# A hybrid SSD and gated-linear-attention trunk: the meta tokens' values from one 32-column operand, and more raw buffers with earlier loads in the Strassen part

## The chip, the cores and the metric

The kernel runs on one core of a Trainium2 chip. The metric is the time of one execution in microseconds of the device. Below, PE is TensorE (PEld its weight loads), DVE is VectorE, ACT is ScalarE, POOL is GpSimd, and SP is SyncE, whose queue issues most of the loads. L966 is line 966 of the kernel.

## The reference, cut to what matters

One layer over 2048 tokens of width 1024, with 16 learned meta tokens ahead of them, in float32:

```python
u = rmsnorm(hres, norm_w)
proj = jnp.einsum('bld,dn->bln', u, w_in)
z, xbc, dt_raw, q, k, v, g_gla, a_lr, merge_g = split_cols(proj, IN_WIDTHS)
...   # convolution and SSD branch: y_ssd
o_m, st_m = gla_chunked(q[:, :m], k[:, :m], v[:, :m], log_a[:, :m], N_META, st0)
o_r, _ = gla_chunked(q[:, m:], k[:, m:], v[:, m:], log_a[:, m:], GLA_CHUNK, st_m)
...   # norm and gate: y_gla
branch_proj = jnp.einsum('blnc,ncd->blnd', branches, w_branch)
gates = jax.nn.sigmoid(merge_g.reshape(b, l, N_BRANCH, D_MODEL))
merged = jnp.sum(gates * branch_proj, axis=2)
return hres + jnp.einsum('bld,de->ble', merged, w_out)
```

After the layer comes a final rmsnorm, and the meta tokens are dropped. Of the meta tokens the gated branch needs only what they leave in its state, `st_m`: for each of the four heads the sum over the 16 tokens of the decayed key times the value.

## The kernel before, in words

**Products.** A float32 number is split into a high and a low part (`h`, `lo`), both of type float32r, and a product is three matmuls: high by high, high by low, low by high. The helper `accum` issues them, at L189, L190 and L191, so nearly every matmul of the kernel carries one of these three lines. A tile is named by its tag: `whl` is a weight split in two, `u` the normalised input split in two.

**First part (to about 1500 us).** Four blocks of 512 tokens. In each block four groups of the SSD branch and four heads of the gated branch are projected and scanned, as generators that PE's program order interleaves. In block 0 the 16 meta tokens ride along. For the values of a head, `gla_values` calls `proj_tok`: for each of eight slices of the inner dimension the four chunks of 128 tokens are the stationary operand, and 256 columns of weights are the moving one. In block 0 a fifth chunk, 128 tokens from token 0 on, goes the same way into bank `pv5` (tag `pt`); only its first 16 rows are read, into `vm`. In `gla_scan` the meta tokens' decayed keys (`kd[:, :META]`) are transposed on PE (L771), copied (L773) and multiplied with `vm` (L785), which gives the state `s_gla`.

**Second part (from about 1504 us).** Seven stages, one after the other: gate 0, branch 0 and branch 1 for the first 1024 tokens (56, 28 and 28 products), the same three for the second 1024, and the output stage (56 products). Each stage is a matrix product by Strassen's scheme in Winograd's form: per column pair `n` seven products, in the order `PS = (1, 2, 6, 7, 5, 3, 4)`, two column pairs at a time, so 1, 1, 2, 2, 6, 6, 7, 7, 5, 5, 3, 3, 4, 4. A product is twelve matmuls of 512 columns (`product`, four slices by three passes). The work around it:

- *Right operands.* Each stage needs 28 tiles, four for each of the seven products. `load_b` (L966) loads a raw tile (tag `br`, 5 buffers, SP's queue), `prep_b` splits it: the high part on ACT (L971), the low part on DVE (L972). DVE's instruction frees the raw buffer.
- *Left operands.* `load_a` (L978) loads four raw tiles per column pair (tag `ar`, 8 buffers, SP's queue); POOL forms their sums (L986 to L989), `prep_a` splits each (ACT L995, DVE L996).
- *Snapshots.* Products 1, 6, 5 and 3 add up in one bank (`psa`). After 1, 6 and 5 ACT copies the running sum out (`sn`, L1012), and PE may go on in that bank only then. Between 1 and 6, and between 6 and 5, three other products lie; between 5 and 3 there is one.

PE's and SP's orders are written out: `at(pos, ...)` puts every load and preparation at a position counted in products, and SP issues in that order, each instruction waiting for its own buffer and holding back all behind it. A stage's right operands are prepared from 12 positions ahead of the stage on, 0.8 positions apart, and loaded 3.2 positions ahead of that. The orders on ACT, DVE and POOL are set by a scheduler, at build time. Besides, SBUF holds 16 KB per partition (the default) as scratch for descriptors of DMAs that POOL issues.

Of the kernel before, what the change touches and what calls it, by code (L numbers as in the profile page):

```python
# [19 lines left out]
NCH = BLK // P  # L20
SG = 4
# [7 lines left out]
NC1 = 6  # L29
# [11 lines left out]
def trunk_kernel(ctx: ExitStack, tc: tile.TileContext, xm, xmt, w_feat, w_tok, w_zm, w_br, w_o,  # L41
                 cf32, cmsk, pvec, fnw, hvec, gw2, out):
    nc = tc.nc
# [84 lines left out]
    wk = first.enter_context(tc.tile_pool(name="wk", bufs=2))  # L128
# [58 lines left out]
    def accum(ps, stat, mov, first, last, **kw):  # L187
        (sh, sl), (mh, ml) = stat, mov
        nc.tensor.matmul(ps, sh, mh, start=first, stop=False, **kw)  # L189
        nc.tensor.matmul(ps, sh, ml, start=False, stop=False, **kw)  # L190
        nc.tensor.matmul(ps, sl, mh, start=False, stop=last, **kw)  # L191
# [10 lines left out]
                    accum(ps[:, :n], (h[:, cs], lo[:, cs]), moving(kt, a, n), kt == 0, kt == KT - 1)  # L202
        return pss

    def proj_tok(key, src, u, starts, banks, width=256, per=2, sub=None):

        nq = KT // per
        opened = set()  # L210
        for q0 in range(0, nq, 2):
            if q0 == nq // 2:
                yield
            ws = [load_w(f"{key}_{q}", src[:, q * per * width:(q + 1) * per * width]) for q in (q0, q0 + 1)]
            for i, ((bk, ps), a) in enumerate(zip(banks, starts)):
                c0 = sub if sub is not None and i >= NCH else 0
                for k2 in range(2 * per):
                    kt = q0 * per + k2
                    h, lo = ws[k2 // per]
                    cs = slice(k2 % per * width + c0, (k2 % per + 1) * width)  # L220
                    accum(ps[:, c0:width], tuple(t[:, kt, a:a + P] for t in u),
                          (h[:, cs], lo[:, cs]), bk not in opened, kt == KT - 1, skip_group_check=True)
                    opened.add(bk)
# [149 lines left out]
    def new_block(b, u):  # L373
        o = Block()
        o.b, o.u = b, u
        o.m0 = META if b == 0 else 0
        o.tt = o.m0 + BLK
        o.segs_all = [(0, o.tt // 2), (o.tt // 2, o.tt // 2)] if b == 0 else [(0, BLK)]
        o.segs_real = [(o.m0, BLK)]
        o.starts = [o.m0 + c * P for c in range(NCH)]  # L380
        o.chunks = ([(0, META)] if o.m0 else []) + [(a, P) for a in o.starts]
        o.ci0 = 1 if o.m0 else 0
        o.nck = len(o.chunks)
        for nm in ("tkd", "tkc", "ntc", "wde", "ecu", "dec"):
            setattr(o, nm, mk(bpool, [P, 5, NH], F32, nm, bufs=1))
        o.cumd = mk(dpool, [NH, BLK], F32, "cumd")
        o.g_all = mk(bpool, [P, GH, META + BLK], F32, "g_all")
        o.alr = mk(bpool, [P, 5, 48], F32, "alr")
        o.mov = lambda kt, a, n: tuple(t[:, kt, a:a + n] for t in u)
        return o  # L390
# [256 lines left out]
    def gla_values(o, h):  # L647
        m0 = o.m0
        vh = mk(wk, [P, NCH, 256], F32R, "tok4", bufs=NT4)
        vl = mk(wk, [P, NCH, 256], F32R, "tok4", bufs=NT4)  # L650
        vm = None
        pss, places = halves_of(pj, "pj")
        if m0:
            vm = mk(wk, [P, 256], F32, "c1", bufs=NC1)[:META]
            pv5 = bank(pt, "pt")
            places.append((2, pv5[:, :256]))
        yield from proj_tok(f"v{h}", w_tok[SG + h], o.u, o.starts + [0] * o.ci0, places)
        if m0:
            nc.scalar.activation(vm, pv5[:META, :256], AF.Copy)
        for r, ps in enumerate(pss):  # L660
            split(*[t[:, 2 * r:2 * r + 2].rearrange("p c f -> p (c f)") for t in (vh, vl)], ps)
        return (vh, vl), vm
# [36 lines left out]
    def gla_scan(o, h, qs, kf, got):  # L699
# [68 lines left out]
        yield  # L768
        if m0:
            ps = bank(pt, "pt")  # L770
            nc.tensor.transpose(ps[:META, :P], kd[:, :META], ident)  # L771
            btm = mk(wk, [P, P], F32, "bt")
            nc.scalar.activation(btm[:META], ps[:META, :P], AF.Copy)  # L773
        ps = bank(pt, "pt")
        for c in range(NCH):
            nc.tensor.transpose(ps[:, c * P:(c + 1) * P], kd[:, m0 + c * P:m0 + (c + 1) * P], ident)
# [5 lines left out]
        yield  # L782
        if m0:
            ps = bank(pc, "pc")
            nc.tensor.matmul(ps[:, :256], btm[:META], got["v"][1], start=True, stop=True)  # L785
            nc.vector.tensor_copy(s_gla[:, h], ps[:, :256])
        level_out(32)
        level_in(8)
# [162 lines left out]
    class Stage:  # L951
# [9 lines left out]
        def load_b(self, p, j):  # L961
            src = {1: lambda j: self.braw(j, 0), 2: lambda j: self.braw(4 + j, 0), 3: lambda j: self.braw(4 + j, 1),
                   4: lambda j: self.sums[1][j][:, 1], 5: lambda j: self.sums[0][j][:, 1],
                   6: lambda j: self.sums[1][j][:, 0], 7: lambda j: self.sums[0][j][:, 0]}[p]
            raw = self.braws[p, j] = mk(rpl, [P, BLK], F32, "br", bufs=5)
            nc.sync.dma_start(raw, src(j))  # L966

        def prep_b(self, p, j):
# [5 lines left out]

        def load_a(self, n):
            def raw(i, j):
                t = mk(rpl, [P, 4, P], F32, "ar", bufs=8)
                nc.sync.dma_start(t, self.araw(n, i, j))  # L978
                return t

            if n not in self.a:
                self.a[n] = raw(0, 0), raw(0, 1), raw(1, 0)
                return
            (a11, a12, a21), a22 = self.a[n], raw(1, 1)
            s1, s2, s4 = [mk(rpl, [P, 4, P], F32, "as", bufs=6) for _ in range(3)]
            nc.gpsimd.tensor_tensor(s1, a21, a22, op=ALU.add)  # L986
            nc.gpsimd.tensor_tensor(s2, s1, a11, op=ALU.subtract)
            nc.gpsimd.tensor_tensor(a21, a11, a21, op=ALU.subtract)
            nc.gpsimd.tensor_tensor(s4, a12, s2, op=ALU.subtract)  # L989
            self.a[n] = {1: a11, 2: a12, 3: s4, 4: a22, 5: s1, 6: s2, 7: a21}  # L990
# [71 lines left out]
    def out_stage():  # L1062
        fns, res, ssq, done = [], {}, {}, set()

        def fetch(n, i, t):
            r0 = (2 * n + i) * P
            res[n, i, t] = r = io()
            nc.sync.dma_start(r, xm[META + r0:META + r0 + P, t * BLK:(t + 1) * BLK])

        def use(n, i, t, ps, snap):  # L1070
            r0 = (2 * n + i) * P
            r = res[n, i, t]
            done.add((n, i, t))
            x = total(ps, snap)
            nc.vector.scalar_tensor_tensor(r, x, 0.5, r, op0=ALU.mult, op1=ALU.add)
            if (n, i) not in ssq:
                ssq[n, i] = mk(spl, [P, 2], F32, "ssf")
            jk = mk(spl, [P, BLK], BF16, "junk", bufs=1)
            nc.scalar.activation(jk, r, AF.Square, accum_out=ssq[n, i][:, t:t + 1])
            if (n, i, 1 - t) in done:  # L1080
                while len(fns) < 2:
                    fns.append(mk(rpl, [P, BLK], F32, "br", bufs=5))
# [13 lines left out]

    stages = []
# [24 lines left out]
    for si, st in enumerate(stages):  # L1122
        for q in range(28):
            p, j = PS[q // 4], q % 4
            pos = begins[si] - 12 + 0.8 * q if si else -0.99 + 0.2 * (q // 4) if q < 16 else 2 * (q // 4 - 4)
            at(pos - (3.2 if si else 0.1), lambda st=st, p=p, j=j: st.load_b(p, j))
            at(pos, lambda st=st, p=p, j=j: st.prep_b(p, j))
    for i, (st, n, p) in enumerate(order):
        if p in USES and st.fetch:
# [108 lines left out]
```

## Time and profile before

| | |
|---|---|
| time, median of 3 runs (lowest, highest) | 2315.93 us (2313.01, 2315.98) |
| profiled execution, its own time | 2308.46 us |
| its span, first to last instruction | 2306.7 us |
| PE busy | 2232.1 us, 97% |
| DVE, ACT, POOL busy | 1609.6, 1121.4, 683.6 us |
| moved by DMA | 515.89 MB, 224 GB/s on average |
| mean granted clock of TensorE | 0.990 |

All durations come from the profiled execution. It took 7.47 us less than the median of the runs; a sum made against its time is carried over to the median by that difference. PE is busy nearly always, so what counts is which matmuls there are, and the few places where PE stands still.

### The profile page before, as it was taken

What the parts mean: (1) busy time and instruction counts of PE and PEld (TensorE: products, weight loads), DVE (VectorE), ACT (ScalarE), POOL (GpSimd) and SP (SyncE); (2) the same over time, 40 slices, a digit from 0 to 9 for tenths busy, and PEclk for the clock granted to TensorE, in tenths of its full rate; (3) what the DMA queues carried; (4) which work ended last, traced back from release to release, by engine and by line L of the source; (5) the groups of instructions that cost most, each with busy time, mean ns of one, the idle gap of its engine ahead of it and who ended that gap; (6) DMA issues with size and microseconds to landing.
All of it is one profiled execution on the core that took longest, in us unless ns stands there. A gap on an engine that the chain in (4) does not pass through costs nothing.

```text
span 2306.7 us, 36436 instructions
## 1 busy us (share of the span) xinstructions
PE 2232.1 (97%) x12631; PEld 1949.0 (84%) x12631; DVE 1609.6 (70%) x3136; ACT 1121.4 (49%) x2508; POOL 683.6 (30%) x675
## 2 busy tenths in 40 slices
PE   6899999999999999999999999989999999999998
PEld 6899988888888989888988898778787788787886
DVE  5786766687775677676578656664779855778966
ACT  5565554454444445444455334454644545554443
POOL 3344433122221222222122100145424264423341
PEclk9999999999999999999999999999999999999999
DMA  7766865667786676786667644465767866778653
GB/s 260 234 220 219 289 229 205 203 204 230 257 284 193 204 223 213 253 286 215 205 216 230 215 163 156 151 224 200 252 238 261 280 215 217 255 255 273 226 186 110
DMA packets 300809, 515.89 MB, mean 224 GB/s; under 512 B 27616, under 2 KB 143584, under 8 KB 300624
## 3 DMA queue, kind: packets, MB, share of 16 engines
q1 hardware_dynamic: 221840, 422.15, 56.5%
q10 hardware_dynamic: 78624, 90.89, 11.2%
q8 instruction: 99, 1.62, 0.3%
q14 instruction: 86, 0.70, 0.1%
q0 software_dynamic: 160, 0.52, 0.1%
HBM read 366.26 MB, written 147.19 MB: 223 GB/s over the span
## 4 chain that ended last, share of the span: by engine, by line
PE 64%; DVE 12%; DMA 12%; issue 6%; ACT 4%; POOL 1%; SPq 1%; ACTq 0%; DVEq 0%; POOLq 0%
PE pj L189 11%; PE pj L191 11%; PE pj L190 11%; PE psa L189 4%; PE psa L190 4%; PE psa L191 4%; DMA acc<-in_xmt 2%; PE psb L190 2%; PE psb L189 2%; PE psb L191 2%; DMA br<-br_t 2%; PE pc L594 2%; PE pc L758 1%; DVE b L972 1%; PE psc L190 1%
## 5 line engine op out<-in xcount | busy, mean ns | idle before, releaser
L189 PE MATMUL pj<-u,whl 128*128 128x512 f32 (+1 forms) x1184 | 446.0, 377 | 9.5 <-ACT acc L504 4.5
L191 PE MATMUL pj<-u,whl 128*128 128x512 f32 (+1 forms) x1184 | 430.7, 364 | 0.8 <-POOL whl L177 0.8
L190 PE MATMUL pj<-u,whl 128*128 128x512 f32 (+1 forms) x1184 | 430.1, 363 | 0.0
L189 PE MATMUL pj<-whl,u 128*128 128x256 f32 (+1 forms) x992 | 288.7, 291 | 2.4 <-ACT u L252 2.2
L191 PE MATMUL pj<-whl,u 128*128 128x256 f32 (+1 forms) x992 | 282.2, 285 | 0.2 <-DVE u L257 0.2
L190 PE MATMUL pj<-whl,u 128*128 128x256 f32 (+1 forms) x992 | 282.0, 284 | 0.0
L189 PE MATMUL psa<-b,a 128*128 128x512 f32 x640 | 254.0, 397 | 16.4 <-ACT sn L1012 16.2
L189 PEld LDWEIGHTS pj<-u,whl 128*128 128x128 f32 x1184 | 224.5, 190 | 48.4 <-ACT acc L504 5.4
L190 PE MATMUL psa<-b,a 128*128 128x512 f32 x640 | 253.1, 395 | 2.0 <-DVE b L972 2.0
L191 PEld LDWEIGHTS pj<-u,whl 128*128 128x128 f32 x1184 | 224.0, 189 | 36.6 <-POOL whl L177 1.0
L190 PEld LDWEIGHTS pj<-u,whl 128*128 128x128 f32 x1184 | 224.8, 190 | 33.3
L191 PE MATMUL psa<-b,a 128*128 128x512 f32 x640 | 252.6, 395 | 0.0
L996 DVE TENSOR_TENSOR a<-ar,a 128x512 fp32r<-128x512 f32 x160 | 148.1, 930 | 84.3 <-ACT a L995 84.1
L80 POOL TENSOR_TENSOR wr<-wr 128x256 f32<-128x256 f32 x80 | 69.4, 868 | 442.7 <-DMA wr<-u 184.4
L177 POOL TENSOR_TENSOR whl<-wr,whl 128x512 fp32r<-128x512 f32 (+1 forms) x100 | 136.5, 1373 | 195.4 <-ACT whl L176 155.5
L189 PEld LDWEIGHTS pj<-whl,u 128*128 128x128 f32 x992 | 189.6, 191 | 4.1 <-ACT u L252 2.3
L191 PEld LDWEIGHTS pj<-whl,u 128*128 128x128 f32 x992 | 189.6, 191 | 0.8 <-DVE u L257 0.8
L190 PEld LDWEIGHTS pj<-whl,u 128*128 128x128 f32 x992 | 189.8, 191 | 0.4
L972 DVE TENSOR_TENSOR b<-br,b 128x512 fp32r<-128x512 f32 x196 | 148.4, 780 | 43.2 <-ACT b L971 43.1
L986 POOL TENSOR_TENSOR as<-ar,ar 128x512 f32<-128x512 f32 x40 | 59.4, 1484 | 396.2 <-DMA ar<-in_w_br 154.2
L508 DVE SCALAR_TENSOR_TENSOR acc<-cin,hcw,acc 128x512 f32<-128x512 f32 (+1 forms) x192 | 159.6, 831 | 13.9 <-ACT acc L504 11.6
L971 ACT ACTIVATE b<-br 128x512 fp32r<-128x512 f32 x196 | 119.3, 626 | 93.4 <-DMA br<-br_t 41.4
(281 smaller groups left out, 5017.7 us busy)
## 6 DMA issues: line engine op xcount, KB each, us to landing
whl<-k_s SPq DMA_DIRECT2D x96, 512.0 KB, 4.3
whl<-k_g SPq DMA_DIRECT2D x96, 512.0 KB, 4.2
whl<-k_v SPq DMA_DIRECT2D x48, 512.0 KB, 4.0
whl<-k_z SPq DMA_DIRECT2D x36, 512.0 KB, 4.1
wr<-in_w_feat SPq DMA_DIRECT2D x64, 256.0 KB, 4.3
k_s<-whl SPq DMA_DIRECT2D x32, 512.0 KB, 3.7
cb<-cumd ACTq DMA_DIRECT2D x64, 256.0 KB, 5.7
k_g<-whl SPq DMA_DIRECT2D x32, 512.0 KB, 3.9
```

The costliest lines, as they stand in the source:

```text
L80: nc.gpsimd.tensor_tensor(o, x, y, op=ALU.subtract)
L177: nc.gpsimd.tensor_tensor(hl[:, 1], raw, hl[:, 0].bitcast(F32), op=ALU.subtract)
L189: nc.tensor.matmul(ps, sh, mh, start=first, stop=False, **kw)
L190: nc.tensor.matmul(ps, sh, ml, start=False, stop=False, **kw)
L191: nc.tensor.matmul(ps, sl, mh, start=False, stop=last, **kw)
L508: nc.vector.scalar_tensor_tensor(acc, cin[:, k:k + tt], hcw[:, ti, k:k + 1], acc, op0=ALU.mult, op1=ALU.add)
L594: nc.tensor.matmul(py[:, h * 64:(h + 1) * 64], dm[:, h], xdt[:, h], start=True, stop=True)
L758: nc.tensor.matmul(ps[:, r * P:(r + 1) * P], kq[:, 2 * r * P:(2 * r + 1) * P], kq[:, (2 * r + 1) * P:(2 * r + 2) * P], start=True, stop=True)
L971: nc.scalar.activation(t[:, 0], raw, AF.Copy)
L972: nc.vector.tensor_tensor(t[:, 1], raw, t[:, 0].bitcast(F32), op=ALU.subtract)
L986: nc.gpsimd.tensor_tensor(s1, a21, a22, op=ALU.add)
L996: nc.vector.tensor_tensor(t[:, 1], src, t[:, 0].bitcast(F32), op=ALU.subtract)
```

## The change

Line numbers below 205 are the same in both; beyond, the changed kernel's are 5 to 13 higher (L971 becomes L984, L995 L1008, L1012 L1025, L966 L979, L978 L991).

```diff
-    def proj_tok(key, src, u, starts, banks, width=256, per=2, sub=None):
+    def proj_tok(key, src, u, starts, banks, width=256, per=2, sub=None, both=None):
...
+                    if both is not None and i >= NCH:
+                        for part in (h, lo):
+                            nc.tensor.matmul(ps[:2 * META], both[:, kt], part[:, cs], start=kt == 0 and part is h,
+                                             stop=kt == KT - 1 and part is lo)
+                        continue
...
+        o.both = None
+        if o.m0:
+            o.both = mk(wk, [P, KT, 2 * META], F32R, "both", bufs=1)
+            for i in range(2):
+                nc.gpsimd.tensor_copy(o.both[:, :, i * META:(i + 1) * META], u[i][:, :, :META].bitcast(F32))
...
-            vm = mk(wk, [P, 256], F32, "c1", bufs=NC1)[:META]
+            vm = mk(wk, [P, 256], F32, "c1", bufs=NC1)[:2 * META]
...
-            nc.scalar.activation(vm, pv5[:META, :256], AF.Copy)
+            nc.scalar.activation(vm, pv5[:2 * META, :256], AF.Copy)
...
-            nc.tensor.transpose(ps[:META, :P], kd[:, :META], ident)
+            kdm = mk(wk, [P, P], F32, "bt")[:, :2 * META]
+            nc.vector.tensor_copy(kdm.rearrange("p (r t) -> p r t", r=2),
+                                  kd[:, :META].unsqueeze(1).to_broadcast([P, 2, META]))
+            nc.tensor.transpose(ps[:2 * META, :P], kdm, ident)
...
-            nc.tensor.matmul(ps[:, :256], btm[:META], got["v"][1], start=True, stop=True)
+            nc.tensor.matmul(ps[:, :256], btm[:2 * META], got["v"][1], start=True, stop=True)
...
-            raw = self.braws[p, j] = mk(rpl, [P, BLK], F32, "br", bufs=5)
+            raw = self.braws[p, j] = mk(rpl, [P, BLK], F32, "br", bufs=8)
...
-                t = mk(rpl, [P, 4, P], F32, "ar", bufs=8)
+                t = mk(rpl, [P, 4, P], F32, "ar", bufs=10)
...
-            at(pos - (3.2 if si else 0.1), lambda st=st, p=p, j=j: st.load_b(p, j))
+            at(pos - (4.4 if si else 0.1), lambda st=st, p=p, j=j: st.load_b(p, j))
...
-    nc = _bacc.Bacc("TRN2", target_bir_lowering=False, num_devices=1)
+    nc = _bacc.Bacc("TRN2", target_bir_lowering=False, num_devices=1, dynamic_dma_scratch_size=2048)
```

**The meta tokens' values.** The high and the low parts of the 16 meta tokens stand side by side in one stationary tile, `both`, of 32 columns, which POOL fills once. Two passes, with the high and the low part of the weights, take the place of three. Rows 0 to 15 of the result belong to the high part, rows 16 to 31 to the low part; they are added by giving the decayed keys twice (a copy on DVE into `kdm`, then the transpose of 32 columns), so that the product with `vm` sums over 32 rows.

On PE, in block 0, half of the values of a head, before. The names are tile<-moving operand,stationary operand; `pt_3064` is `pv5`:

```order
L189 MATMUL pt_3064<-whl_3065,u_255 128x256
L190 MATMUL pt_3064<-whl_3065,u_255 128x256
L191 MATMUL pt_3064<-whl_3065,u_255 128x256
L189 MATMUL pt_3064<-whl_3072,u_255 128x256
L190 MATMUL pt_3064<-whl_3072,u_255 128x256
```

and after, with the matmuls of the last chunk of real tokens ahead of it:

```order
L189 MATMUL pj_3065<-whl_3075,u_255 128x256
L190 MATMUL pj_3065<-whl_3075,u_255 128x256
L191 MATMUL pj_3065<-whl_3075,u_255 128x256
L223 MATMUL pt_3067<-whl_3068,both_372 32x256 x4
L223 MATMUL pt_3067<-whl_3075,both_372 32x256 x4
```

Of each half's twelve matmuls of 128 rows (three for each of four slices) eight of 32 rows are left; with eight halves, 96 become 64.

**The scratch and the buffers.** The scratch shrinks to 2 KB per partition. The raw right operands get 8 buffers, the raw left ones 10, and right operands are loaded 4.4 positions ahead of their preparation in all stages but the first.

On SP, around the end of gate 0, before. `br_t` and `in_w_br` belong to the next stage, branch 0; the `br` rows here are its right operands 10 to 13 (from 0), the `ar` rows the left ones of its first two column pairs:

```order
L978 DMA ar_18630<-in_w_br 128x512
L978 DMA ar_18632<-in_w_br 128x512
L978 DMA ar_18634<-in_w_br 128x512
L966 DMA br_18639<-br_t_2_182 128x512
L966 DMA br_18657<-br_t_3_183 128x512
L978 DMA ar_18678<-in_w_br 128x512
L966 DMA br_18693<-br_t_0_176 128x512
L978 DMA ar_18695<-in_w_br 128x512
L978 DMA ar_18697<-in_w_br 128x512
L978 DMA ar_18699<-in_w_br 128x512
L978 DMA ar_18718<-in_w_br 128x512
L966 DMA br_18730<-br_t_1_177 128x512
```

and after:

```order
L979 DMA br_18588<-br_t_2_182 128x512
L979 DMA br_18611<-br_t_3_183 128x512
L991 DMA ar_18613<-in_w_br 128x512
L991 DMA ar_18615<-in_w_br 128x512
L991 DMA ar_18617<-in_w_br 128x512
L979 DMA br_18638<-br_t_0_176 128x512
L991 DMA ar_18659<-in_w_br 128x512
L979 DMA br_18668<-br_t_1_177 128x512
L991 DMA ar_18676<-in_w_br 128x512
L991 DMA ar_18678<-in_w_br 128x512
L991 DMA ar_18680<-in_w_br 128x512
L979 DMA br_18682<-br_t_2_178 128x512
```

Right operands 10 and 11 moved ahead of the first three left ones, number 13 ahead of the last four; number 14 now stands where 13 stood, less one left operand.

On ACT, at the same place, before. The last row is the snapshot after product 5 of the last column pairs of gate 0; `a_18687` is the left operand of product 4 of the last of them:

```order
L971 ACTIVATE b_3235_18750<-br_18639 128x512
L971 ACTIVATE b_3238_18758<-br_18657 128x512
L995 ACTIVATE a_18687<-ar_18357 128x512
L971 ACTIVATE b_3243_18783<-br_18693 128x512
L995 ACTIVATE a_18727<-ar_18630 128x512
L971 ACTIVATE b_3245_18804<-br_18730 128x512
L971 ACTIVATE b_3250_18831<-br_18753 128x512
L1012 ACTIVATE sn_18674<-psa_18457 128x512
```

and after (`a_18670` is what `a_18687` was):

```order
L984 ACTIVATE b_3245_18741<-br_18611 128x512
L1008 ACTIVATE a_18670<-ar_18336 128x512
L984 ACTIVATE b_3249_18764<-br_18638 128x512
L984 ACTIVATE b_3252_18787<-br_18668 128x512
L1008 ACTIVATE a_18710<-ar_18613 128x512
L984 ACTIVATE b_3256_18812<-br_18682 128x512
L984 ACTIVATE b_3260_18833<-br_18716 128x512
L1025 ACTIVATE sn_18655<-psa_18438 128x512
```

The snapshot stands behind one right operand more than before (16 in place of 15).

More of the change, by code (lines that the diff above doesn't have):

```diff
@@ L653, in gla_values @@
         if m0:
-            vm = mk(wk, [P, 256], F32, "c1", bufs=NC1)[:META]
+            vm = mk(wk, [P, 256], F32, "c1", bufs=NC1)[:2 * META]
             pv5 = bank(pt, "pt")
             places.append((2, pv5[:, :256]))
-        yield from proj_tok(f"v{h}", w_tok[SG + h], o.u, o.starts + [0] * o.ci0, places)
+        yield from proj_tok(f"v{h}", w_tok[SG + h], o.u, o.starts + [0] * o.ci0, places, both=o.both)
         if m0:
-            nc.scalar.activation(vm, pv5[:META, :256], AF.Copy)
+            nc.scalar.activation(vm, pv5[:2 * META, :256], AF.Copy)
         for r, ps in enumerate(pss):
@@ L770, in gla_scan @@
             ps = bank(pt, "pt")
-            nc.tensor.transpose(ps[:META, :P], kd[:, :META], ident)
+            kdm = mk(wk, [P, P], F32, "bt")[:, :2 * META]
+            nc.vector.tensor_copy(kdm.rearrange("p (r t) -> p r t", r=2),
+                                  kd[:, :META].unsqueeze(1).to_broadcast([P, 2, META]))
+            nc.tensor.transpose(ps[:2 * META, :P], kdm, ident)
             btm = mk(wk, [P, P], F32, "bt")
-            nc.scalar.activation(btm[:META], ps[:META, :P], AF.Copy)
+            nc.scalar.activation(btm[:2 * META], ps[:2 * META, :P], AF.Copy)
         ps = bank(pt, "pt")
@@ L1081, in use @@
                 while len(fns) < 2:
-                    fns.append(mk(rpl, [P, BLK], F32, "br", bufs=5))
+                    fns.append(mk(rpl, [P, BLK], F32, "br", bufs=8))
                     nc.sync.dma_start(fns[-1], fnw[:, (len(fns) - 1) * BLK:len(fns) * BLK].to_broadcast([P, BLK]))
```

## The prediction, written before the changed kernel was run

> **What bounds the kernel.** First the page's busy times, to see which engine sets the pace:
>
> ```profile
> PE 2232.1 (97%) x12631; PEld 1949.0 (84%) x12631; DVE 1609.6 (70%) x3136; ACT 1121.4 (49%) x2508; POOL 683.6 (30%) x675
> ```
>
> PE has 2306.7 - 2232.1 = 74.6 us of idle time in the whole span. A change gains by removing matmuls, or idle time of PE. Next I cut the span into stretches of 50 us (stretch, PE busy and count, the other engines, granted clock, DMA share, GB/s). In the second part six of sixteen stand out:
>
> ```profile
> 1500.00:1550.00 50.00, 44.60 (x181) 35.39 (x182) 33.55 (x51) 31.43 (x58) 17.84 (x16) 0.90 0.72 237
> ...
> 1650.00:1700.00 50.00, 47.35 (x203) 38.75 (x202) 39.16 (x45) 26.03 (x46) 23.99 (x15) 0.97 0.73 252
> 1700.00:1750.00 50.00, 48.34 (x214) 39.67 (x213) 41.44 (x56) 24.52 (x43) 13.45 (x8) 1.00 0.71 236
> ...
> 1800.00:1850.00 50.00, 47.03 (x200) 38.42 (x199) 41.31 (x60) 25.96 (x47) 14.09 (x9) 0.97 0.84 283
> ...
> 1950.00:2000.00 50.00, 47.17 (x201) 38.56 (x200) 39.80 (x51) 30.03 (x55) 16.86 (x12) 0.97 0.82 276
> ...
> 2100.00:2150.00 50.00, 45.23 (x188) 36.86 (x187) 41.78 (x61) 23.13 (x42) 12.86 (x8) 0.93 0.89 287
> ```
>
> The last five each hold one stop of PE: 2.65, 1.66, 2.97, 2.83 and 4.77 us. They lie at the seams between stages. Four of them also lose granted clock, 3, 3, 3 and 7% of 50 us, so 1.5, 1.5, 1.5 and 3.5 us. Who ends the stops, by the waits of PE from 1440 us on (total, times, longest):
>
> ```profile
> PE psa L189 <- ACT sn L1012: 16.2, 6, 4.8
> ```
>
> Six stops, all for ACT's snapshot; the sixth is 16.2 - 14.88 = 1.3 us, in the first stretch. Why is ACT late? The chain of waits at the first seam (start, us, what):
>
> ```profile
> 1648.06 1.80 DVE a L996
> 1649.87 0.33 SPq L978
> ...
> 1650.25 0.42 SPq L966
> ...
> 1650.72 3.51 DMA br<-br_t
> ...
> 1654.26 0.63 ACT b L971
> 1654.89 0.49 ACT sn L1012
> ...
> 1655.42 0.80 PE psa L189
> 1656.22 0.43 PE psa L190
> ...
> 1658.75 0.23 PE psa L190
> ```
>
> Read upwards: PE waits for the snapshot, which stands on ACT behind a right operand that has not landed; its load was issued at 1650.72, since SP stood at a left operand's load (L978) until DVE freed a raw buffer (L996, itself late, being behind ACT). SP's and ACT's own rows say how long (the bracket is the idle time before):
>
> ```profile
> 1643.42 6.77 SPq L978 DMA_DIRECT2D ar<-in_w_br  x4
> ...
> 1653.57 1.32 ACT L971 ACTIVATE b<-br 128x512 fp32r<-128x512 f32 x2 [4.22 <-DMA br<-br_t]
> ...
> 1735.47 0.63 ACT L971 ACTIVATE b<-br 128x512 fp32r<-128x512 f32 x1 [3.55 <-DMA br<-br_t]
> ...
> 1808.08 0.63 ACT L971 ACTIVATE b<-br 128x512 fp32r<-128x512 f32 x1 [5.12 <-DMA br<-gate_t]
> ...
> 1969.74 1.27 ACT L971 ACTIVATE b<-br 128x512 fp32r<-128x512 f32 x2 [4.85 <-DMA br<-br_t]
> ...
> 2123.88 0.63 ACT L971 ACTIVATE b<-br 128x512 fp32r<-128x512 f32 x1 [3.82 <-DMA br<-out_t]
> ```
>
> At every seam one such wait of ACT (4.22, 3.55, 5.12, 4.85, 3.82 us) comes shortly before PE's stop, and all but the last are longer than the stop (2.65, 1.66, 2.97, 2.83, 4.77). SP's waits in total:
>
> ```profile
> SPq L966 <- DVE b L972: 126.1, 93, 14.7
> ...
> SPq L978 <- DVE a L996: 102.0, 33, 12.3
> ```
>
> SP holds for a raw right operand's buffer 93 times and for a left one's 33 times. So the loop is: full rings stop SP, SP's order delays right operands, ACT waits, and ACT's lateness frees the rings later.
>
> **The change, part by part.**
>
> *Two passes for the meta tokens.* 96 matmuls become 64. What one costs is its distance to the next, not its duration:
>
> ```profile
> 297.31 0.28 PE L189 MATMUL pt<-whl,u 128*128 128x256 f32 x1
> ...
> 298.61 0.28 PE L191 MATMUL pt<-whl,u 128*128 128x256 f32 x1
> ```
>
> Twelve of them, eleven distances in 1.30 us: 0.118 us each. The moving side stays at 256 columns, so I keep 0.118 us for those left: 32 x 0.118 = 3.8 us less. PE hardly stops there, so the 3.8 us lie on the path. Bounds: 0 if the chunks after it then wait for weights, 96 x 0.118 - 64 x 0.059 = 7.6 us if a stationary tile of 32 columns halved the distance; nothing in the trace shows that, so I take 3.8.
>
> *What it adds.* Four copies of 128x32 on DVE, two casts of 128 elements per partition on POOL. Nearest rows:
>
> ```profile
> L232 DVE TENSOR_SCALAR rstd<-ssq 128x4 f32<-128x4 f32 x32 | 5.2, 164 | 3.4 <-ACT junk L610 2.0 <-ACT junk L862 1.3
> L506 POOL COPY tails<-cin 128x3 f32<-128x3 f32 x64 | 19.8, 309 | 163.4 <-ACT cin L503 157.2 <-DVE c L606 5.9
> L177 POOL TENSOR_TENSOR whl<-wr,whl 128x288 fp32r<-128x288 f32 x8 | 6.8, 860 | 26.2 <-ACT whl L176 24.4 <-DMA wr<-in_w_zm 1.8
> ```
>
> A copy costs at least 0.16 us, and PE's transpose now waits for it: 4 x 0.16 = 0.7 us if none is hidden, 0 if all are. The heads' transposes come later than the keys are ready in most cases, so I take 0.2. The casts lie between 0.31 and 0.86 us each, 1.7 us at most together; POOL's row at that place has 1.8 us of idle time (26.2 idle, 1.8 of it for a raw weight's load), so 0, with 0 to 1.7 as ends. If that cover is gone, the weights' splits behind them are late.
>
> *Buffers, order and lead of the right operands.* A product is twelve matmuls:
>
> ```profile
> 1672.01 0.39 PE L189 MATMUL psa<-b,a 128*128 128x512 f32 x1
> ...
> 1674.73 0.39 PE L189 MATMUL psc<-b,a 128*128 128x512 f32 x1
> ```
>
> so 2.72 us, one position. A load of right operand q waits for the preparation of q-5, planned 0.8 x 5 = 4.0 positions before that of q; at a lead of 3.2 that leaves 0.8 positions, 2.2 us, for DVE to be late before SP stands. After: 0.8 x 8 - 4.4 = 2.0 positions, 5.4 us. For left operands, 8 buffers make the last load of a column pair wait for the last preparation (product 4) two pairs back; with 10 it is the second load of the second pair that waits, for the preparation of product 4 one pair earlier. And the load itself is issued 1.2 positions, 3.3 us, earlier in SP's order, ahead of left operands that stood before it. Landing takes:
>
> ```profile
> ar<-in_w_feat SPq DMA_DIRECT2D x64, 256.0 KB, 5.2
> br<-br_t SPq DMA_DIRECT2D x64, 256.0 KB, 5.0
> ar<-in_w_br SPq DMA_DIRECT2D x64, 256.0 KB, 5.3
> ```
>
> so a lead of 4.4 x 2.72 = 12.0 us leaves 7 us of slack where 8.7 us left 3.7. Per seam, 3.3 us of earlier issue (and SP's stand of up to 4 us, by the row of 6.77 us for four loads, which take some 0.4 us each when free) against stops of 1.66 to 4.77 us. Against it: ACT's order now has one to four more right operands ahead of the deciding snapshot, each 0.5 us of ACT when it has landed.
>
> What I take: first seam (1655) and fourth (1971), the same gate-to-branch pattern, gone with their clock, 2.65 + 1.5 + 2.83 + 1.5 = 8.5. The 1.3 us at 1541, behind the first stage's right operands, gone. Second (1738), where most right operands are moved ahead of the snapshot: half, 0.8. Third (1814), with DMA at 283 GB/s: 3.5 of 4.5. Fifth (2130), at 287 GB/s, the highest, and where the wait is shorter than the stop: 5 of 8.3. Together 19.1 us of at most 16.2 + 8.0 = 24.2; the lower end is 0.
>
> The clock's part is from the rows above: after the stop of 2.65 us matmuls start 0.43 us apart, later 0.23; after that of 1.66 us the stretch shows 1.00. The Trainium skill, TensorE: Matmul & The Clock Gate, Part 1, has the clock halve after an idle window of about 3.4 us. By that only the fifth stop would carry a clock loss, and the sum would be 3 x 1.5 = 4.5 us smaller; the trace disagrees, with stops of 2.65, 2.97 and 2.83 us that do carry it, and the sum goes by the trace.
>
> *What is late next.* The left operands. Their load is 2.5 positions, 6.8 us, ahead of their first use and lands in 5.3: 1.5 us of slack. Two more right operands ahead of them, at the 283 GB/s of a seam 0.93 us each for 262144 bytes, take 1.9 us, so 0.4 us too late. The price lies between 0 and 0.4 us at each of six seams; I take 1.0 in all.
>
> *The scratch.* POOL issues only two transfers:
>
> ```profile
> y<-gg POOLq DMA_DIRECT2D x2, 256.0 KB, 2.8
> ...
> POOL as L986 <- DMA ar<-in_w_feat: 96.5, 8, 30.4
> ```
>
> and after them, around 1508 us, it waits up to 30.4 us for left operands. If the smaller scratch made it wait, that covers it: 0, with 0 to 2.8 as ends.
>
> **Sum.** -3.8 + 0.2 - 19.1 + 1.0 = -21.7 us. Against the profiled execution's own 2308.46 us (span 2306.7 and 1.8 around it) that is 2286.8; that execution was 7.5 us faster than the median of the runs, 2315.93, so for the median I say 2294.2 us, a ratio of 0.9906.
>
> **Rivals.**
>
> *Half of the stops stay.* ACT's order was made anew, and puts each right operand where a build-time estimate had it landed. If that is too early by as much as before, the snapshot waits as before, and only the stands of SP are gained. For it: ACT's order moved by one or two right operands at most seams, about the 1.2 positions of the lead. Against: the deciding wait at the first seam came from a full ring. Gain 8 to 16, so 2300 to 2308 us.
>
> *No stop is gained, and only the two passes count.* The right operands wait at the same lanes: at the third and fifth seam DMA is busy 0.84 and 0.89 of the time, and no byte is saved. For it these rows, against it 0.71 to 0.73 at the first two. Gain 0 to 8, most likely 3.8: about 2312 us.
>
> *Slower: the left operands take over.* If 6.8 us of lead don't do behind up to four more right operands (4 x 0.93 = 3.7 us, less 1.5 of slack: 2.2 us late), PE stops at six seams for 2.2 us and loses 1.5 us of clock: 22 us. If the old stops go too it is a draw at 2315.93 - 3.8 - 24.2 + 22 = 2310; it becomes a loss once fewer than 18 of the 24.2 us go, and with half of them kept it is 2315.93 - 3.8 - 12 + 22 = 2322 us. Against it: in the trace ACT waits for right operands nearly always, for left ones hardly.
>
> **Numbers.** Most stops gone (gain 16 to 28): 0.60. Half (8 to 16): 0.20. Passes alone (0 to 8): 0.13. Left operands take over: 0.07. Runs of the kernel before lie within 3 us, 0.13%, so 0.2% (4.6 us) is about what a measurement tells from no change. Faster by more: 0.80 and a little of the third case, 0.82; within: 0.11; slower: 0.07. The range covers the first two cases, 2288 to 2308, and a run's scatter of 1 to 3 us: 2285 to 2309.
>
> **What would show it.** Right: 64 matmuls with `both`, 0.118 us apart; PE's waits for L1025 at 2 to 7 us in place of 16.2; SP's waits for L985 below half of 126.1; no row of ACT's above 3 us for a right operand at 1650 and 1965; clock of 1.00 there. Wrong: the same rows with `ar` where `br` stood, POOL or ACT idle for left operands before PE's stops; or ACT's waits as long as before with SP free, which would say that the transfers, not the rings, were late.

## The result: slower by 0.6%, and the profile after

| | before | changed |
|---|---|---|
| median | 2312.59 us (6 runs, 2304.8 to 2315.98) | 2325.62 us (6 runs, 2322.48 to 2331.33) |
| ratio to before, 95% interval | | 1.0060 (1.0044 to 1.0076) |
| profiled execution, span | 2306.7 us | 2320.7 us |
| first matmul of the second part | 1504.59 us | 1501.93 us |
| second part, first to last of its matmuls | 792.2 us | 808.9 us |

I had forecast 2294.2 us, with a range of 2285 to 2309. In the two profiled executions the first part ended 2.7 us earlier and the second took 16.7 us more. The matmuls there are the same, so PE must stand still or run slower for longer. The waits of PE from 1508 us on (total, times, longest):

```profile
PE psa L189 <- ACT sn L1025: 20.5, 7, 5.6
PE psb L189 <- DVE sn L1036: 8.8, 5, 2.3
```

That is 29.3 us in place of 16.2. The second row is new: PE now also waits for a bank (`psb`) that DVE has not yet added to its snapshot (L1036). The stretches of 50 us show where (same columns as before):

```profile
1650.00:1700.00 50.00, 44.73 (x190) 36.51 (x190) 35.50 (x47) 22.07 (x40) 15.30 (x11) 0.93 0.69 231
1700.00:1750.00 50.00, 47.30 (x208) 38.52 (x207) 41.97 (x54) 24.35 (x44) 13.06 (x8) 1.00 0.62 214
...
1800.00:1850.00 50.00, 45.68 (x199) 36.83 (x199) 42.73 (x58) 24.29 (x45) 16.13 (x11) 1.00 0.80 280
1850.00:1900.00 50.00, 44.63 (x187) 36.46 (x186) 24.28 (x26) 19.74 (x35) 33.46 (x29) 0.93 0.47 155
...
1950.00:2000.00 50.00, 44.36 (x184) 36.11 (x183) 38.61 (x46) 29.97 (x55) 17.09 (x12) 0.93 0.81 276
...
2100.00:2150.00 50.00, 48.48 (x214) 39.85 (x213) 43.40 (x56) 21.41 (x39) 16.82 (x12) 1.00 0.86 284
```

The first and the fourth seam, which I had called gone, now hold stops of 5.27 and 5.64 us in place of 2.65 and 2.83, and at 1860 there is one of 5.37 us that the kernel before did not have. The third and the fifth seam gained: stops of 2.25 us in place of 2.97, and of 1.51 and 1.61 in place of 4.77, with a clock of 1.00; the 1.3 us in the first stage are gone. Yet at the branch stages the right operands are in time, as forecast: ACT waits for branch operands 7.8 us in place of 41.4 (for gate operands 14.2 in place of 14.1), and the stands of SP for a left operand's buffer (102.0 us) are gone.

```profile
ACT b L984 <- DMA br<-br_t: 7.8, 7, 1.6
```

So who is late? DVE at the first seam (start, us, what; the bracket is the idle time before):

```profile
1639.05 3.00 DVE L985 TENSOR_TENSOR b<-br,b 128x512 fp32r<-128x512 f32 x3 [1.43 <-ACT b L984]
1641.97 1.78 DVE L1009 TENSOR_TENSOR a<-ar,a 128x512 fp32r<-128x512 f32 x1
1643.68 1.78 DVE L985 TENSOR_TENSOR b<-br,b 128x512 fp32r<-128x512 f32 x1
1645.38 1.78 DVE L1009 TENSOR_TENSOR a<-ar,a 128x512 fp32r<-128x512 f32 x1
1647.09 3.48 DVE L985 TENSOR_TENSOR b<-br,b 128x512 fp32r<-128x512 f32 x2
1650.48 1.77 DVE L1009 TENSOR_TENSOR a<-ar,a 128x512 fp32r<-128x512 f32 x1
1652.18 2.35 DVE L985 TENSOR_TENSOR b<-br,b 128x512 fp32r<-128x512 f32 x2
1654.45 0.68 DVE L1036 TENSOR_TENSOR sn<-sn,psb 128x512 f32<-128x512 f32 x1
1655.05 0.68 DVE L1009 TENSOR_TENSOR a<-ar,a 128x512 fp32r<-128x512 f32 x1
```

DVE is never idle from 1639.05 on, and from 1641.97 on each preparation takes 1.78 us, one every 1.70 us; from 1655 the same instruction takes 0.68, one every 0.60. POOL in that time, first and last of its eight sums of left operands, which follow each other without a pause:

```profile
1640.03 1.47 POOL L999 TENSOR_TENSOR as<-ar,ar 128x512 f32<-128x512 f32 x1 [8.11 <-DMA ar<-in_w_br]
...
1651.66 1.71 POOL L1002 TENSOR_TENSOR as<-ar,as 128x512 f32<-128x512 f32 x1
```

DVE is slow while POOL forms sums. In the kernel before the same change of pace came later, with POOL's first sum, and with pauses in which DVE waited for ACT:

```profile
1644.52 0.69 DVE L996 TENSOR_TENSOR a<-ar,a 128x512 fp32r<-128x512 f32 x1 [0.31 <-ACT a L995]
1648.06 1.79 DVE L996 TENSOR_TENSOR a<-ar,a 128x512 fp32r<-128x512 f32 x1
1654.23 2.37 DVE L972 TENSOR_TENSOR b<-br,b 128x512 fp32r<-128x512 f32 x2 [0.99 <-ACT b L971]
```

```profile
1647.56 1.74 POOL L986 TENSOR_TENSOR as<-ar,ar 128x512 f32<-128x512 f32 x1 [13.28 <-DMA ar<-in_w_br]
```

In the changed kernel, behind these preparations stands the snapshot's addition (L1036); behind that ACT, and behind ACT PE:

```profile
1655.16 0.63 ACT L1043 ACTIVATE sn<-sn 128x512 f32<-128x512 f32 x1 [6.83 <-DVE sn L1036]
...
1656.21 0.58 ACT L1025 ACTIVATE sn<-psa 128x512 f32<-128x512 f32 x1
```

```profile
1656.85 0.79 PE L189 MATMUL psa<-b,a 128*128 128x512 f32 x1 [5.27 <-ACT sn L1025]
```

Counted over the instructions of DVE in the second part, 58 took over 1.5 us before, and 90 take so long now; in both kernels some 94% of their time lies beside a POOL instruction, of the ones under 0.75 us some 12 and 9%. The larger rings let right and left operands land early and together, so that DVE's preparations and POOL's sums now fall into the same 13 us, ahead of a snapshot.

### The profile page after: what moved, and what is told of

Its sections match the earlier page's. It is cut to its first block, busy times and chain, and to the rows that moved or that the text cites. A ratio compares the mean times of both kernels' runs of the same rounds, so it can differ in the third digit from the quotient of the medians.

```text
span 2320.7 us, 36409 instructions
## 1 busy us (share of the span) xinstructions
PE 2231.7 (96%) x12599; PEld 1946.3 (84%) x12599; DVE 1634.6 (70%) x3140; ACT 1116.6 (48%) x2508; POOL 680.6 (29%) x677
## 4 chain that ended last, share of the span: by engine, by line
PE 69%; DVE 12%; DMA 10%; issue 3%; ACT 3%; POOL 1%; SPq 1%; ACTq 0%; DVEq 0%; POOLq 0%
PE pj L189 11%; PE pj L191 11%; PE pj L190 11%; PE psa L189 5%; PE psa L190 5%; PE psa L191 5%; PE psb L189 2%; PE psb L190 2%; PE psb L191 2%; DMA acc<-in_xmt 2%; PE pc L768 2%; PE pc L604 1%; DVE b L985 1%; PE psc L189 1%; PE psc L190 1%
## 5 line engine op out<-in xcount | busy, mean ns | idle before, releaser
L1009 DVE TENSOR_TENSOR a<-ar,a 128x512 fp32r<-128x512 f32 x160 | 161.8, 1019 | 69.1 <-ACT a L1008 68.7
L80 POOL TENSOR_TENSOR wr<-wr 128x256 f32<-128x256 f32 x80 | 67.3, 842 | 443.4 <-DMA wr<-u 185.7
L985 DVE TENSOR_TENSOR b<-br,b 128x512 fp32r<-128x512 f32 x196 | 157.6, 840 | 23.5 <-ACT b L984 23.5
L189 PEld LDWEIGHTS psa<-b,a 128*128 128x128 f32 x640 | 122.3, 191 | 50.3 <-ACT sn L1025 24.0
```

The lines of the kernel that those rows point to most:

```text
L80: nc.gpsimd.tensor_tensor(o, x, y, op=ALU.subtract)
L985: nc.vector.tensor_tensor(t[:, 1], raw, t[:, 0].bitcast(F32), op=ALU.subtract)
L1009: nc.vector.tensor_tensor(t[:, 1], src, t[:, 0].bitcast(F32), op=ALU.subtract)
```

## The experiments

Theory A: DVE, slowed by POOL's sums, is what the snapshots wait for. Rivals: the loads are late by SP's order or by the lanes, that is the DMA engines (B); the rings, the buffers of one tag, cost as such (C, R); the plan puts too many right operands ahead of the snapshots (P); a store that waits for POOL stands ahead of one (S). Each kernel was timed against the kernel before on the same chip, and the ratio is to those times. "Second part", "stops" (those of over 0.4 us, from 20 us into the second part on) and "slow" (DVE instructions of over 1.5 us) are from the one profiled execution. The second part scatters from one execution to the next: e1's is written as the one of the kernel before, and took 6 us more.

| kernel | right, left ring | lead | sums on | median us | ratio (95%) | second part | stops | slow |
|---|---|---|---|---|---|---|---|---|
| before | 5, 8 | 3.2 | POOL | 2312.6 | 1 | 792.2 | 16.2 | 58 |
| changed | 8, 10 | 4.4 | POOL | 2325.6 | 1.0060 (1.0044, 1.0076) | 808.9 | 29.4 | 90 |
| e1 | 5, 8 | 3.2 | POOL | 2309.3 | 0.9986 (0.9971, 1.0000) | 798.2 | 19.3 | 64 |
| e2 | 8, 10 | 3.2 | POOL | 2317.3 | 1.0028 (1.0017, 1.0039) | 803.0 | 26.4 | 78 |
| e3 | 8, 8 | 4.4 | POOL | 2315.2 | 1.0013 (0.9999, 1.0026) | 799.5 | 21.2 | 62 |
| e4 | 5, 8 | 4.4 | POOL | 2303.5 | 0.9966 (0.9951, 0.9980) | 790.9 | 15.4 | 64 |
| e5 | 8, 16 | 4.4 | none | 2286.4 | 0.9889 (0.9868, 0.9910) | 769.8 | 2.3 | 0 |
| e6 | 5, 10 | 4.4 | POOL | 2315.4 | 1.0021 (1.0007, 1.0036) | 800.3 | 22.6 | 73 |
| e7 | 8, 8 | 3.2 | POOL | 2310.0 | 0.9990 (0.9973, 1.0006) | 797.0 | 20.7 | 60 |
| e8 | 5, 8 | 5.6 | POOL | 2302.0 | 0.9965 (0.9951, 0.9979) | 788.4 | 14.2 | 67 |
| e9 | 8, 10 | 4.4 | POOL | 2316.3 | 1.0013 (0.9997, 1.0029) | 801.9 | 23.6 | 84 |
| e10 | 8, 10 | 4.4 | DVE | 2299.1 | 0.9942 (0.9922, 0.9963) | 779.9 | 9.1 | 0 |
| e11 | 5, 8 | 5.6 | DVE | 2308.5 | 0.9976 (0.9960, 0.9992) | 792.4 | 18.8 | 0 |
| e12 | 8, 10 | 4.4 | DVE | 2290.5 | 0.9907 (0.9891, 0.9923) | 768.4 | 2.1 | 0 |

All but the kernel before have the two passes. e1, e4, e8 and e11 have the old scratch of 16 KB.

**e1, the two passes alone.** Edit: the diff's part on the meta tokens, nothing else.

> The kernel before with the two passes alone (old scratch, rings of 5 and 8, lead 3.2). All theories: the second part as before, so six stops for the snapshot, 16 us in all (12 to 20). The changed kernel reached the second product of the second part at 1504.75 us, the kernel before at 1507.40, so 2.7 us faster: about 2310 us against 2312.6. If the passes gain nothing, 2312.6; if the whole 13 us of loss came from them, 2325.

Measured: 2309.3 us, 0.14% less with an interval that ends at no change. As expected; the passes did not cost the 13 us. Against e1 the changed kernel is 16.3 us slower by the medians, so that is the price of rings, lead and scratch.

**e2, the old lead; e3, eight left buffers; e4, the lead with the old rings.** Edits against the changed kernel: e2 the first line, e3 the second, e4 the last two (each `+` line), with the old scratch.

```diff
-            at(pos - (4.4 if si else 0.1), ...)
+            at(pos - (3.2 if si else 0.1), ...)
...
-                t = mk(rpl, [P, 4, P], F32, "ar", bufs=10)
+                t = mk(rpl, [P, 4, P], F32, "ar", bufs=8)
...
-            raw = self.braws[p, j] = mk(rpl, [P, BLK], F32, "br", bufs=8)
+            raw = self.braws[p, j] = mk(rpl, [P, BLK], F32, "br", bufs=5)
```

> The changed kernel with the old lead of 3.2 for the right operands (rings of 8 and 10, small scratch, two passes kept). Theory A (DVE is the one that is late: supplied with right operands while POOL forms its sums, it needs 1.78 us in place of 0.69 for each, and the snapshots stand behind): the earlier lead is what fed DVE during POOL's sums, so DVE has fewer slow instructions than the 90 of the changed kernel, and the time lies at 2305 to 2315. Theory B (the left operands are late, because SP has right operands ahead of them): the old order gives the left operands back their place, waits of POOL for left operands move back, 2303 to 2312. Theory C (the rings themselves, not the lead): as the changed kernel, 2320 to 2328.

> The changed kernel with 8 raw buffers for left operands in place of 10; the order of instructions stays the same on PE, SP and DVE. Theory A in its form with the ring: two more buffers let POOL form the sums of two column pairs in one go (eight sums, 13 us, at 1640 to 1653), and DVE is slow all that time; with 8 the second four sums come later, slow DVE instructions fall from 90 towards 60, the stop of 5.3 us at the first seam falls under 3, 2312 to 2320. If the ring of 10 has no part in it: 2322 to 2328, 90 slow instructions.

> The kernel before with the two passes and the lead of 4.4, old rings (5 and 8) and old scratch. A right operand's buffer comes free 4.0 positions ahead, so SP stands at nearly every right operand. Theory A: DVE is still fed no earlier than the ring of 5 allows, so few slow instructions more than before (60 to 75), stops about as before: 2308 to 2320. Theory B (the order on SP delays left operands): SP's stands now also delay left operands, more than in the changed kernel: 2322 to 2340.

Measured: e2 2317.3, above what A and B gave it and under C's range; the lead is 8 us of the loss beside the large rings, no more. e3 2315.2 with 62 slow instructions, as A's form with the ring said, though its first stop is 3.4 us, not under 3. e4 2303.5, less than I expected of it: with the old rings the longer lead and the passes together gain 0.34% against before. B in its form with SP's order falls here: the order is the changed kernel's, and e4 is faster. What costs is the rings, or what they let in.

**e5, no sums of left operands.** The raw tiles stand in their place, so this part of the computation is left out. The six buffers of the sums go to the raw left ring, which has 16.

```diff
-            nc.gpsimd.tensor_tensor(s1, a21, a22, op=ALU.add)
...
-            self.a[n] = {1: a11, 2: a12, 3: s4, 4: a22, 5: s1, 6: s2, 7: a21}
+            self.a[n] = {1: a11, 2: a12, 3: a12, 4: a22, 5: a21, 6: a11, 7: a21}
```

> The changed kernel without POOL's sums of left operands: raw tiles stand in their place, so this part of the computation is left out; the six buffers of the sums go to the raw left ring (16), and ACT's and DVE's orders put as many right operands ahead of each snapshot as in the changed kernel. Theory A (POOL's sums slow DVE from 0.69 to 1.78 us an instruction, and the snapshots stand behind DVE): slow DVE instructions fall from 90 to under 20, stops from 29 us to under 10, 2288 to 2302 us. Theory B (the loads are late, by SP's order or by the lanes): no byte is saved and the order on SP is the same, so stops of 20 us and more stay, 2312 to 2326.

Measured: 2286.4 us, no slow instruction, and one wait of PE's left from 1515 us on. This speaks for A: the bytes and SP's order are the changed kernel's. The left ring is not, but SP doesn't stand for left buffers in the changed kernel either; e10 has the ring of 10.

```profile
PE psa L189 <- ACT sn L1020: 2.3, 1, 2.3
```

DVE's groups in the second part, busy and mean ns, first the changed kernel, then e5 (its lines are 5 lower from `load_a` on):

```profile
L985 DVE TENSOR_TENSOR b<-br,b 128x512 fp32r<-128x512 f32 x190 | 154.0, 845 | 23.5 <-ACT b L984 23.5
...
L1036 DVE TENSOR_TENSOR sn<-sn,psb 128x512 f32<-128x512 f32 x80 | 54.6, 683 | 55.1 <-ACT sn L1025 36.2 <-PE psb L191 18.6
```

```profile
L985 DVE TENSOR_TENSOR b<-br,b 128x512 fp32r<-128x512 f32 x194 | 127.7, 690 | 26.6 <-ACT b L984 24.9 <-DMA io<-g 1.1
L1031 DVE TENSOR_TENSOR sn<-sn,psb 128x512 f32<-128x512 f32 x80 | 54.8, 685 | 74.9 <-ACT sn L1020 50.3 <-PE psb L191 24.5
```

The preparation, with both inputs in SBUF, falls from 845 to 690 ns; the snapshot's addition, with one input in PSUM, has 683 and 685. None of these additions took over 0.69 us, though in the changed kernel 14 of them, and in the kernel before 35, lie beside POOL's sums: POOL does not touch them. The Trainium skill, SBUF — State Buffer, section Who interferes with whom, states just this: a DVE instruction with two SBUF inputs contends with a GpSimd instruction that reads SBUF, and one with at most one SBUF input, outside the 2-port perf modes, doesn't. The traces agree on both halves, and add the price here: 1.70 us an instruction in place of 0.60.

**e6, the old right ring; e7, three right buffers more; e8, a lead of 5.6.**

> The changed kernel with the old ring of 5 raw right operands (lead 4.4 and 10 left buffers kept, small scratch); against the run of passes and lead with the old rings (2303.5 us) it has two left buffers more and the same order on SP and DVE. If ten left buffers cost 10 us by themselves, as between 8 and 10 beside a right ring of 8: 2311 to 2316 and 75 to 90 slow DVE instructions. If they only cost when the ring of 8 keeps SP from standing at right operands, so that POOL's sums come early (1640 in place of 1646 us): 2301 to 2308, 60 to 70 slow ones.

> The two passes, 8 right and 8 left buffers, small scratch, the old lead of 3.2. Against the run of the passes alone it has only three right buffers more; ACT's plan has, summed over all snapshots, 43 more right operands ahead of them than before (73 at a lead of 4.4 with this ring, 22 at 4.4 with the ring of 5). Theory P (what costs is how many right operands the plan puts ahead of the snapshots): between 2309.3 and 2315.2, so 2311 to 2314. Theory R (a larger right ring as such, by filling the lanes or DVE's time): 2314 to 2318, no better than at 4.4. If the larger ring helps once the lead is the old one: under 2306.

> The two passes, the old rings (5 and 8) and scratch, and a lead of 5.6 in place of 4.4. The ring of 5 frees a buffer 4.0 positions ahead, so at 4.4 and at 5.6 SP stands for nearly every right operand, and the larger lead only moves more of them ahead of left operands. Theory A: DVE is fed no earlier, so 2300 to 2308, as at 4.4 (2303.5); the plan has 38 more right operands ahead of snapshots than before, 22 at 4.4, so by theory P some 2 us more, 2305. Theory B (left operands behind right ones on SP): slower than at 4.4, 2308 to 2318.

Measured: e6 2315.4 with 73 slow instructions, nearer the first of its two cases: ten left buffers cost 12 us beside the small right ring too (against e4). e7 2310.0, against e1 2309.3: the larger right ring with the smaller scratch costs next to nothing at the old lead, less than P and R gave it. e8 2302.0, as A said. P does not hold: with 22 and 38 more right operands ahead of the snapshots e4 and e8 are faster than e1, which has none more, and e5, with the changed kernel's 73, is the fastest so far.

**e9, a store moved behind two snapshots.** In the three kernels with ten left buffers timed so far (the changed one, e2, e6) PE stops for 5.4 to 7.1 us some 359 us into the second part; in no other. There, in the changed kernel, ACT stands at a store of a late sum of POOL's:

```profile
1850.20 1.67 ACT L1008 ACTIVATE a<-ar 128x512 fp32r<-128x512 f32 x3
1859.22 0.54 ACTq L962 DMA_DIRECT2D br_t<-io  x1
1859.80 0.60 ACT L1025 ACTIVATE sn<-psa 128x512 f32<-128x512 f32 x1 [7.93 <-POOL io L80]
```

PE's stop follows at once:

```profile
1860.45 0.80 PE L189 MATMUL psa<-b,a 128*128 128x512 f32 x1 [5.37 <-ACT sn L1025]
```

POOL, in order too, forms left operands' sums ahead of what the store waits for:

```profile
1855.58 1.70 POOL L1000 TENSOR_TENSOR as<-as,ar 128x512 f32<-128x512 f32 x1
1857.25 1.25 POOL L1001 TENSOR_TENSOR ar<-ar,ar 128x512 f32<-128x512 f32 x1
1858.47 0.72 POOL L80 TENSOR_TENSOR io<-io,io 128x256 f32<-128x256 f32 x1
```

On ACT the plan for ten buffers has this store directly ahead of the snapshot, the one for eight has it behind. The edit puts one late sum a position later:

```diff
-    spots = [g + 9 + 5 * k for g in begun_at for k in range(8)]
+    spots = [g + 9 + 5 * k + (1 if g and not k else 0) for g in begun_at for k in range(8)]
```

> The changed kernel with one late sum of POOL's (the first one beside the second gate stage) planned one position later; the orders of PE, SP and DVE stay, and on ACT two stores of that sum move from directly ahead of two snapshots to behind them. Theory S (ten left buffers cost because the plan puts a store that waits for POOL ahead of the snapshot: in all three runs with ten buffers PE stops 5.4 to 7.1 us about 359 us into the second part, in none with eight): this stop goes with its clock, 7 to 9 us less, 2316 to 2319 us. Rival (the stop is POOL's lateness itself, or left operands that are late): it stays or another of the same size takes its place, 2322 to 2328.

Measured: 2316.3 us, and no stop between 338 and 478 us into the second part. S holds: some 9 of the changed kernel's 13 us were this store. e6's trace has the same row on ACT, [9.66 <-POOL io L80], and a stop of 7.07 us behind it, which would explain most of its 12 us; e6 without that store was not run.

**e10 and e11, the sums on DVE.** Edit: `nc.gpsimd.tensor_tensor` to `nc.vector.tensor_tensor` in `load_a`, four lines; e10 on the changed kernel, e11 on e8.

> The changed kernel with the sums of left operands on DVE in place of POOL, nothing left out. Theory A: 152 sums of some 0.69 us give DVE 105 us more, and 99 us of slowness go (90 instructions by 1.10 us), so DVE is as busy as before, but evenly; few instructions of 1.78 us are left (only beside late sums, under 20), and the stops fall to 5 to 15 us: 2295 to 2310. Rival (DVE has too much work at the seams whatever its pace, or stands for left operands that have not landed): stops of 25 us and more, 2320 to 2335.

> The two passes, the old rings (5 and 8) and scratch, a lead of 5.6, and the sums of left operands on DVE. Theory A: without POOL's sums its stops of 14 us fall under 8; from 2302 us without the sums on DVE to 2288 to 2298, the fastest kernel with the whole computation. Rival (DVE too full or standing for left operands): 2303 to 2320.

Measured: e10 2299.1 us, no slow instruction, 9 us of stops: with the sums, 109 us of DVE's time in the second part, the changed kernel is faster than before by 0.58%. DVE is busy no longer for it, 1629.7 us in the whole span in place of 1634.6: standing beside POOL's sums had cost it as much as forming them. The stretches of the first, second and fourth seam have no stop at all, and the fourth moves 313 GB/s, more than any seam's stretch of the kernel before (287):

```profile
1650.00:1700.00 50.00, 50.00 (x222) 41.44 (x221) 40.72 (x66) 29.90 (x54) 0.00 (x0) 1.00 0.83 289
1700.00:1750.00 50.00, 50.00 (x222) 41.23 (x222) 39.74 (x65) 25.10 (x45) 0.00 (x0) 1.00 0.61 215
...
1950.00:2000.00 50.00, 50.00 (x223) 41.39 (x222) 41.05 (x65) 32.37 (x60) 4.15 (x4) 1.00 0.90 313
```

So the lanes were not the bound, against that rival of the prediction. e11, with the old rings, came to 2308.5: my 2288 to 2298 was wrong. It has no slow instruction either, and 18.8 us of stops, at the seams where the kernel before has them; DVE, with the sums in its order, now itself stands for left operands (16.9, 14.4 and 13.1 us by its waits; in e10 6.6, 7.9 and 10.5). So taking POOL's sums away is not enough. e10 differs from it in rings, lead and scratch; that the rings are what removes the stops is likely, since SP stands 84.5 us for left buffers in e11 and not at all in e10, but they were not changed alone.

**e12, both.** e10 with the first late sum of each half a position later (`+ (0 if k else 1)` at the same place), so that no store stands directly ahead of a snapshot there.

> The changed kernel with the sums of left operands on DVE, and the first of POOL's late sums beside each gate stage planned one position later, so that no store that waits for POOL stands directly ahead of a snapshot at these two places. Theory S: of the 9 us of stops that the sums on DVE left, the two of 4.5 and 2.7 us go with their clock (1.5 us each at most): 7 to 10 us less than 2299 us, so 2289 to 2293, some 20 us and 0.9% under the kernel before. Rival (POOL's lateness shows at another place): 2296 to 2302.

Measured: 2290.5 us, 0.93% under the kernel before. It is the fastest kernel with the whole computation. PE's waits from 1515 us on:

```profile
PE psa L189 <- ACT sn L1025: 2.1, 3, 1.1
```

## Why the prediction was wrong, step by step

**The two passes: right in kind, not resolved in size.** The new matmuls stand 0.115 us apart (eight in 0.92 us, next start 289.92), as the 0.118 I took; the range's upper end, half the distance, falls.

```profile
282.33 0.28 PE L784 MATMUL pt<-cst,bt 128*32 128x128 f32 x1 [1.22 <-DVE bt L782]
...
289.00 1.08 PE L223 MATMUL pt<-whl,both 128*32 128x256 f32 x8
289.92 1.04 PE L640 MATMUL pt<-cst,tok 128*128 128x128 f32 x8
```

The copies cost 1.2 us at the first head (0.6 in e1's trace) and nothing at the other three, where I took 0.2 and bounded by 0.7. Net 2.7 us by these traces, 0.14% by e1.

**Rings and lead: the mechanism right, the sum wrong.** ACT's waits for right operands went, none over 3 us at the two seams that I named; SP's stands for them fell to 84.9 us, not below half of 126.1. The term of -19.1 us came out as +16.7 us in the trace, 13.1 of them waits, the rest mostly lost clock, and as +16.3 by the medians against e1. The step that failed is "What is late next". I looked for it among the loads and named the left operands, at 1.0 us. Late was DVE, and it was in rows that I had quoted: the chain at the first seam has "1648.06 1.80 DVE a L996", the sum over SP's order counted it only as lateness that holds SP, and nowhere did I ask why the same instruction took 0.69 us elsewhere. My slack of 2.0 positions "for DVE to be late" was spent by eight instructions at 1.10 us more.

**A part not costed at all** was the store: the plan for ten buffers moved a row of ACT's that I had not compared, since I compared only snapshots and operands. e9 gives it 9 of the 22 us that lie between e4 and the changed kernel.

**The gain was there.** e12 has the changed kernel's passes, rings, lead and scratch and comes to 2290.5 us, 22.3 under its kernel before; I had said 21.7 less. So the stops could be removed with these rings as I had reckoned, but only once DVE is not held by POOL's sums and no store stands directly ahead of the snapshots. That the two sizes agree is luck in part: e12 has stops of 2.1 us left of the 16.2, where I had reckoned with 5 us of stops and clock left.

**The scratch** cost nothing that shows: e7, with the small one and a right ring of 8, is 0.7 us above e1; it was not changed alone. **The rivals:** the one that ended slower, at 2322, came near by its time but not by its cause; no left operand's landing ends a stop of PE's directly. It had 0.07.

**What stays open.** With POOL's sums in place, the right ring of 8 at a lead of 4.4 (e3) is 12 us slower than that of 5 (e4), with no more slow instructions (62 and 64). e3's trace shows how PE's stop at the first seam comes about, and it is the way of the kernel before. SP, no longer stopped at right operands, runs on to the left ones and stands there, behind a slow DVE (in all 138.8 us against 89.3 in e4); the right operands behind them are late, and the snapshot stands behind these on ACT:

```profile
1638.45 8.25 SPq L991 DMA_DIRECT2D ar<-in_w_br  x3
...
1653.65 0.63 ACT L984 ACTIVATE b<-br 128x512 fp32r<-128x512 f32 x1 [3.00 <-DMA br<-br_t]
1654.19 0.58 ACT L1025 ACTIVATE sn<-psa 128x512 f32<-128x512 f32 x1
```

The second and the fourth seam have the same rows there (2.77 and 3.29 us). So a slow DVE holds the snapshots in two ways, by its own addition and by the buffers that it frees late. How much of the 12 us this is, and why the same ring costs next to nothing at the old lead (e7), was not tried apart.

## What to carry to other kernels

When one kind of instruction shows two durations, find what runs beside the longer of them before moving work toward it: here POOL's sums nearly tripled each of DVE's. More buffers and earlier loads don't only remove waits; they decide which engines work at the same time, and an order fixed at build time can put the snapshots behind the work that this slows. After a change of rings, read the whole order of an in-order engine that PE depends on, stores too: one that waits for POOL ahead of a snapshot cost 9 us.

## What the runs showed of the hardware

**The clock after a stop** does not go by the stop's length alone. In e4 a stop of 2.17 us is followed by matmuls 0.43 us apart for some 3 us; in e3 one of 3.41 us by matmuls 0.23 us apart.

```profile
1844.82 0.80 PE L189 MATMUL psa<-b,a 128*128 128x512 f32 x1 [2.17 <-ACT sn L1025]
1845.41 0.63 PE L190 MATMUL psa<-b,a 128*128 128x512 f32 x1
1845.83 0.63 PE L191 MATMUL psa<-b,a 128*128 128x512 f32 x1
```

```profile
1654.82 0.50 PE L189 MATMUL psa<-b,a 128*128 128x512 f32 x1 [3.41 <-ACT sn L1025]
1655.15 0.40 PE L190 MATMUL psa<-b,a 128*128 128x512 f32 x1
1655.39 0.39 PE L191 MATMUL psa<-b,a 128*128 128x512 f32 x1
```

The fourteen traces hold 64 stops of over 1.4 us from 20 us into the second part on. None of the 17 up to 2.11 us is followed by such slow matmuls, all 24 from 3.43 us on are, and of the 23 between 17 are. The slow ones need not follow at once: in e11, after a stop of 3.29 us that ends at 1551.76, matmuls start 0.23 us apart until 1553.26 and 0.43 us apart from 1553.63 to 1556.62.

**The first part's time scatters.** Its end lies between 1492.7 and 1513.9 us over the thirteen profiled executions with the two passes, whose first part is written the same. So the 2.7 us between two traces prove little, the kernel before alone ran between 2303.9 and 2321.9 us, and the 0.2% that I gave as what a measurement can tell was read from runs that happened to lie close.
